# Hybrid decoder layer on one core: the weight loads on GpSimd's queue, and the 32x32 inverses on 128 partitions

## The chip, the cores and the metric

The kernel runs on one core of one Trainium2 chip, as a single launch. The metric is the device time of one execution in microseconds (us). Engine names are those of the profile: PE is TensorE (PEld its weight loads), DVE is VectorE, ACT is ScalarE, POOL is GpSimd, SP is SyncE. "SPq" and "POOLq" are the sequencers of SP and POOL, which issue DMAs in the order of their instruction streams.

## The reference

One layer over 2048 tokens of width 1024, in float32:

```python
h = _rmsnorm(x, norm1_w)
proj = h @ w_in                       # 2048 HGRN2 columns, then 1792 RWKV-7 columns
o_hg = _hgrn2_mixer(q_raw, f_raw, i_raw, g_raw, lb, norm_w)     # 4 heads of 128, chunks of 64
rw_p = rw_p + (_token_shift(rw_p) - rw_p) * rw_shift_mu
o_rw = _rwkv7_mixer(r, k, v, wd, ad, gd, ...)                   # 8 heads of 64
x = x + concat([o_hg, o_rw]) @ w_out
x = x + _conv_ffn(_rmsnorm(x, norm2_w), w_up, conv_w, conv_b, w_down)   # d_ff 2816
return _rmsnorm(x, final_norm_w)
```

RWKV-7 updates a 64x64 state per token, `S = S diag(w) + (S a) b^T + v k^T`. The kernel works it out in chunks of 64 tokens, which needs the inverse of a unit triangular matrix for each chunk and head. HGRN2 is a gated linear recurrence, `S = diag(f) S + k v^T`, also worked out in chunks.

## The kernel before, in words

Phase 1 (function `phase1`) goes from x to the mixers' outputs and through the output projection for the first three of four blocks of 512 tokens. Phase 2 takes the last block's projection and the ConvFFN. The change touches phase 1 alone.

Phase 1 weaves three generators into one program. `dense` does the projections: for each block, 30 jobs of 128 columns of `w_in` (tile `pj`, lines 259 to 261), each 8 steps along the contraction, and each step three matmuls, since a float32 product is made from a high and a low part (`mm3`, `split`). It also does the norms, and for blocks 0 to 2 `out_block`, the product with `w_out`. `rw_stream` runs eight "supers" (`rw_super`, one for each block and half of the RWKV heads). `hg_stream` runs sixteen HGRN units (`hg_unit`, one for each block and head). After each step of the two mixers, `fill` adds dense work to the program. A scheduler then fixes the order of the instructions on each engine when the program is built. On the chip each engine, and each queue of DMA issues, goes through its own list in order and waits where a semaphore tells it to.

Weights. In block 0 a job loads two 256 KB pieces of `w_in` (tile `wraw`, line 550, four buffers), ACT and DVE split them into `wh` and `wl` (lines 243 and 244, four buffers each), and the halves are stored in DRAM as `Win` by POOL's queue (line 553). In blocks 1 to 3 a job loads four pieces of `Win` back (line 557). `out_block` loads `w_out` in 256 KB pieces into the same four `wraw` buffers (tile `woraw`, line 382), and splits them. All these loads are issued by SP's queue, as are the small transfers below, the mixers' outputs `oT` of blocks 0 to 2 (lines 918 and 1039), and the loads and stores of x. The outputs of block 3 are issued by POOL's queue (`last_dma`).

The inverse. A super holds 64 triangular 32x32 blocks: two halves of heads (u), two chunks of a pair (e), two diagonal blocks of a chunk (q), four pairs (b), two heads (h). DVE leaves them in tile `M` (line 708). Eight DMAs of 32 KB write them to DRAM as `Ed` (line 721), and one reads them back with a matrix to each of 64 partitions (`E`, line 723). DVE inverts by forward substitution: 31 steps of a multiply and an add (lines 774 and 776, tiles `etmp` and `Ti`), in which row j is taken into the rows below, over j + 1 columns. DVE then makes a transposed copy `TiT` (line 781), both go to DRAM as `Td` (lines 780 and 782), and twelve DMAs read them back: four into `TZ` (line 792) and eight into `TTs` (line 789). That is 23 DMAs a super. PE uses the result in three stages of small matmuls: `z` (line 800), `z2` (line 813) and `qus` (line 826). From `qus` ACT copies Q into `M` and the rest into `UV`; then come line 851 (needs Q), lines 867 and 874 (need `UV`), the chain over chunks (line 885), and the end (lines 895 to 918).

The HGRN unit. `scaled(l)` runs for levels 0 to 6 with four DVE multiplications each (lines 944 to 949): the odd halves of q times `Pf`, the even halves of k times `Sf`, and the updates of `Sf` and `Pf`. `Sf` starts as ones (line 937). Lines 965 and 1007 are matmuls on what they make.

Of the kernel before, what the change touches and what calls it, by code (L numbers as in the profile page):

```python
# [18 lines left out]
P = 128  # L19
# [42 lines left out]
def tile_layer(ctx, tc, consts, x, norm1_w, w_in, hg_lb_logits, hg_norm_w, rw_shift_mu, rw_w0, rw_w2,  # L62
# [200 lines left out]
    def phase1(c1):  # L263
# [23 lines left out]

        done = {"rw1": 0, "rw2": 0, "hg": 0}
# [77 lines left out]
        def out_block(nb, oh=None, ol=None, then=None):  # L366


            for i2 in range(2):
                for dh in range(2):  # L370
                    accs = [bank("pj") for _ in range(2)]
                    for k in range(KD):
# [9 lines left out]
                        dma(raw, w_out[0, k * P:(k + 1) * P, dh * 512:dh * 512 + 512])  # L382
# [115 lines left out]
        def dense():  # L498
# [45 lines left out]
            def load(i):  # L544
                if i < len(cols) and i not in loaded:
                    ws, ct = [], cols[i] // P
                    for k2 in range(2):
                        if i < NCOL:
                            raw = wp.tile([P, 4, P], F32, tag="wraw", name="wraw", bufs=4)
                            dma(raw, w_in[0, k2 * 512:k2 * 512 + 512, cols[i]:cols[i] + P].rearrange("(k p) c -> p k c", p=P))  # L550
# [3 lines left out]
                        else:  # L554
                            ws.append(tuple(wp.tile([P, 4, P], F32R, tag="w" + c, name="w" + c, bufs=4) for c in "hl"))
                            for c in range(2):
                                dma(ws[k2][c].bitcast(F32), Win[ct][k2][c])
# [71 lines left out]
        def rw_super(nb, s_):  # L629
# [68 lines left out]
            for j in range(2):  # L698
                for u in U:
# [7 lines left out]
                    for h in range(2):  # L707
                        V.tensor_mul(M[:, u, :, 2 * j:2 * j + 2, h, :].rearrange("p e b t -> p b e t"),
                                     s1[:, h].rearrange("p (b e t) -> p b e t", e=2, t=P),
                                     s1m.unsqueeze(1).unsqueeze(1).broadcast_to([P, 2, 2, P]))  # L710
# [4 lines left out]
            Td = dp.tile([2, 64, 32, 32], F32, tag="Td", name="Td", bufs=2)  # L715
# [37 lines left out]
            for b, h, e, u in quads():  # L753
                kr, c0, sl = 64 - er0(e), col0(u, e), (b * 2 + h) * 64
                TE.matmul(lv[c0:c0 + 64, u, sl:sl + 64], M[kr:kr + 64, u, e, b, h, 0:64],
# [9 lines left out]
            n = 64  # L765
            Ti = rp.tile([P, 32, 32], F32, tag="Ti", name="Ti")
            V.memset(Ti[0:n], 0.0)
            V.memset(Ti[0:n].rearrange("m a b -> m (a b)")[:, 0:1024:33], 1.0)
            yield
            for j in range(31):  # L770
                nr, ncol = 31 - j, j + 1
                tmp = rp.tile([P, 272], F32, tag="etmp", name="etmp")
                tv = tmp[0:n, 0:nr * ncol].rearrange("m (a b) -> m a b", b=ncol)
                V.tensor_mul(tv, E[0:n, j, j + 1:32].unsqueeze(2).broadcast_to([n, nr, ncol]),
                             Ti[0:n, j, 0:ncol].unsqueeze(1).broadcast_to([n, nr, ncol]))
                V.tensor_add(Ti[0:n, j + 1:32, 0:ncol], Ti[0:n, j + 1:32, 0:ncol], tv)
                if j % 4 == 3:
                    yield
            TiT = rp.tile([P, 32, 32], F32, tag="E", name="TiT")
            dma(Td[0], Ti[0:n])  # L780
            V.tensor_copy(TiT[0:n], Ti[0:n].rearrange("m a b -> m b a"))
            dma(Td[1], TiT[0:n])
            TZ = tile_("XH", [2, 2, 4, 2, 32], "TZ")
            for u in U:
                for e in range(2):
                    r0 = er0(e)
# [5 lines left out]
                    dma(TZ[r0:r0 + 32, 0, u].rearrange("p b h t -> p (b h) t"),  # L792
                        Td[0, m0:m0 + 8].rearrange("m s t -> s m t"))
# [3 lines left out]
            for b, h, e, u in quads():  # L797
                r0 = er0(e)
                c0, sl = r0 + 32 - 32 * u, u * 256 + (b * 2 + h) * 32
                TE.matmul(z[c0:c0 + 32, 0, sl:sl + 32], M[r0:r0 + 32, u, e, b, h, 32:64],  # L800
# [705 lines left out]
```

## Time and profile before

| what | value |
|---|---|
| median of 3 runs (lowest to highest) | 2757.54 us (2757.54 to 2757.74) |
| the profiled execution: its time, its span | 2750.25 us, 2748.5 us |
| its mean granted TensorE clock | 0.982 |
| instructions | 47939 |

A view that groups instructions has line, engine, operation, names (out<-in) and count, then busy time in us and the mean ns of one, then the idle time before them and what ended it. A view of waits has who waited for whom, the total in us, the number of waits, and the longest. Each engine's busy time in a stretch is in us; "PEclk" there is the granted clock as a share of full speed. Line numbers are those of the kernel before; the changed kernel's are one to five higher.

### The profile page before, as it was taken

How to read it: one execution, taken by the hardware profiler on the slowest of the kernel's cores; microseconds unless marked ns; L12 is line 12 of the kernel's file. 1: busy time of each engine (PE TensorE's matmuls, PEld its weight loads, DVE VectorE, ACT ScalarE, POOL GpSimd, SP SyncE). 2: the span in 40 equal slices, each digit the busy share in tenths (PEclk: the TensorE clock that was granted, in tenths of full speed). 3: DMA queues.
4: the chain of work that ended last, by engine and by line, in shares of the span. 5: the costliest groups of instructions: out<-in, count | busy, mean ns of one | idle time of the engine just before them, and what ended most of it. 6: DMA issues, size and time to landing. Idle time of an engine off the chain costs nothing.

```text
span 2748.5 us, 47939 instructions
## 1 busy us (share of the span) xinstructions
PE 2645.1 (96%) x18059; PEld 2108.0 (77%) x18059; DVE 1964.0 (71%) x3697; ACT 1329.2 (48%) x2124; POOL 75.7 (3%) x144
## 2 busy tenths in 40 slices
PE   8999999989999899999989999998999999999998
PEld 6777777767777667778668788886888888777887
DVE  5868666585576765757567789988997787667656
ACT  5455342544534444343346754555545455445544
POOL 3211000000000000000000000000000000000000
PEclk9999999989999999999999999999999999999999
DMA  9555544345653456743584467746662224999865
GB/s 302 197 163 169 166 133 127 118 133 183 209 168 120 140 158 216 239 167 121 152 279 145 126 206 260 243 143 225 220 221 75 91 86 157 312 329 311 287 195 184
DMA packets 396029, 513.68 MB, mean 187 GB/s; under 512 B 73503, under 2 KB 200853, under 8 KB 395797
## 3 DMA queue, kind: packets, MB, share of 16 engines
q1 hardware_dynamic: 385137, 476.49, 53.9%
q0 software_dynamic: 10592, 34.11, 3.4%
q8 instruction: 142, 2.33, 0.4%
q14 instruction: 90, 0.74, 0.1%
q10 hardware_dynamic: 68, 0.02, 0.0%
HBM read 373.12 MB, written 137.36 MB: 186 GB/s over the span
## 4 chain that ended last, share of the span: by engine, by line
PE 60%; DVE 7%; DMA 5%; ACT 2%; issue 2%; SPq 1%; DVEq 0%; ACTq 0%
PE ua L261 5%; PE ua L259 5%; PE ua L260 5%; PE pj L259 5%; PE pj L260 4%; PE pj L261 4%; PE ud L259 3%; PE ud L260 3%; PE ud L261 3%; PE da L260 2%; PE da L261 2%; PE da L259 2%; PE db L260 2%; PE db L259 2%; PE db L261 2%
## 5 line engine op out<-in xcount | busy, mean ns | idle before, releaser
L259 PE MATMUL pj<-hh,wh 128*128 128x512 f32 x960 | 401.8, 419 | 0.8 <-DVE xh L398 0.6
L261 PE MATMUL pj<-hh,wl 128*128 128x512 f32 x960 | 379.7, 396 | 0.4 <-DMA wl<-Win191l 0.4
L260 PE MATMUL pj<-hl,wh 128*128 128x512 f32 x960 | 379.7, 396 | 0.0
L259 PE MATMUL ua<-Bh,uwh 128*128 128x512 f32 x704 | 278.7, 396 | 14.9 <-ACT uwh L243 14.1
L261 PE MATMUL ua<-Bh,uwl 128*128 128x512 f32 x704 | 276.3, 393 | 0.3 <-DVE uwl L244 0.3
L260 PE MATMUL ua<-Bl,uwh 128*128 128x512 f32 x704 | 276.1, 392 | 0.0
L259 PEld LDWEIGHTS pj<-hh,wh 128*128 128x128 f32 x960 | 181.3, 189 | 53.4 <-issue 12.4
L260 PEld LDWEIGHTS pj<-hl,wh 128*128 128x128 f32 x960 | 181.4, 189 | 40.3 <-issue 6.0
L261 PEld LDWEIGHTS pj<-hh,wl 128*128 128x128 f32 x960 | 180.9, 188 | 39.6 <-issue 0.7
L243 ACT CAST uwh<-uraw 128x512 fp32r<-128x512 f32 x220 | 134.5, 618 | 140.9 <-PE ua L260 71.4
L243 ACT CAST dah<-draw 128x512 fp32r<-128x512 f32 x151 | 93.8, 621 | 184.6 <-PE da L260 50.5
L244 DVE TENSOR_TENSOR uwl<-uraw,uwh 128x512 fp32r<-128x512 f32 x220 | 147.3, 688 | 46.9 <-ACT uwh L243 46.8
L244 DVE TENSOR_TENSOR dal<-draw,dah 128x512 fp32r<-128x512 f32 x151 | 104.3, 690 | 104.9 <-ACT dah L243 104.6
L259 PEld LDWEIGHTS ua<-Bh,uwh 128*128 128x128 f32 x704 | 133.4, 190 | 43.7 <-ACT uwh L243 14.7
L261 PEld LDWEIGHTS ua<-Bh,uwl 128*128 128x128 f32 x704 | 133.3, 189 | 30.1 <-DVE uwl L244 2.2
L260 PEld LDWEIGHTS ua<-Bl,uwh 128*128 128x128 f32 x704 | 133.7, 190 | 27.2
L259 PE MATMUL ud<-Bh,uwh 128*128 128x512 f32 x352 | 137.8, 392 | 1.9 <-DVE cv L1357 1.9
L261 PE MATMUL ud<-Bh,uwl 128*128 128x512 f32 x352 | 137.1, 389 | 0.0
L260 PE MATMUL ud<-Bl,uwh 128*128 128x512 f32 x352 | 137.0, 389 | 0.0
L260 PE MATMUL da<-dbl,dah 128*128 128x512 f32 x340 | 134.2, 395 | 0.7 <-DVE dbl L244 0.2
L261 PE MATMUL da<-dbh,dal 128*128 128x512 f32 x340 | 133.2, 392 | 0.0
L259 PE MATMUL da<-dbh,dah 128*128 128x512 f32 x340 | 128.3, 391 | 1.6 <-ACT dbh L243 1.5
(434 smaller groups left out, 5792.2 us busy)
## 6 DMA issues: line engine op xcount, KB each, us to landing
uraw<-in_w_up_dram SPq DMA_DIRECT2D x176, 256.0 KB, 3.2
woraw<-in_w_out_dram SPq DMA_DIRECT2D x96, 256.0 KB, 3.5
draw<-Sg SPq DMA_DIRECT2D x88, 256.0 KB, 3.5
draw<-Tw SPq DMA_DIRECT2D x88, 256.0 KB, 3.7
gd<-y SPq DMA_DIRECT2D x86, 256.0 KB, 2.9
xt<-x1d SPq DMA_DIRECT2D x32, 512.0 KB, 5.3
draw<-gd SPq DMA_DIRECT2D x63, 256.0 KB, 5.0
draw<-in_w_down_dram SPq DMA_DIRECT2D x63, 256.0 KB, 5.2
```

Source lines behind the costliest of these rows:

```text
L243: S.copy(hi, src)
L244: V.tensor_sub(lo, src, hi.bitcast(F32))
L259: TE.matmul(acc, lh, rh, start=first, stop=False, skip_group_check=skip)
L260: TE.matmul(acc, lh, rl, start=False, stop=False, skip_group_check=skip)
L261: TE.matmul(acc, ll, rh, start=False, stop=last, skip_group_check=skip)
```

## The change

It has four parts.

1. The loads of `w_in`, `Win` and `w_out` in phase 1 are issued by GpSimd's queue (`wload`) in place of SP's: 60 of `wraw`, 360 of `Win` and 96 of `woraw`.
2. The inverse runs on 128 partitions. Partitions 0 to 63 hold the even columns of the 64 inverses, partitions 64 to 127 the odd ones; `E` is loaded twice. A step still spans the same rows, but j // 2 + 1 columns in place of j + 1. `M` has its axes u and e exchanged, so that one DMA takes both u. There are 4 DMAs to `Ed`, 2 to `E`, 1 of `Ti`, 2 of `TiT`, 4 to `TZ`, 4 to `TTs`: 17 a super in place of 23. ACT makes the transposed copy in place of DVE.
3. After `qus`, ACT copies all of Q into `M` first, and then `UV`. Before, both were mixed.
4. In level 0 of an HGRN unit `Sf` is all ones, so two of the four multiplications are copies; ACT makes them. `Sf`'s memset writes half as many elements.

```diff
+        wload = nc.gpsimd.dma_start
...
-                        dma(raw, w_out[0, k * P:(k + 1) * P, dh * 512:dh * 512 + 512])
+                        wload(raw, w_out[0, k * P:(k + 1) * P, dh * 512:dh * 512 + 512])
...
-                            dma(raw, w_in[0, k2 * 512:k2 * 512 + 512, cols[i]:cols[i] + P].rearrange("(k p) c -> p k c", p=P))
+                            wload(raw, w_in[0, k2 * 512:k2 * 512 + 512, cols[i]:cols[i] + P].rearrange("(k p) c -> p k c", p=P))
...
-                                dma(ws[k2][c].bitcast(F32), Win[ct][k2][c])
+                                wload(ws[k2][c].bitcast(F32), Win[ct][k2][c])
...
-            for u in U:
-                for e in range(2):
-                    for q in range(2):
-                        r0 = er0(e) + 32 * q
-                        m0 = u * 32 + (e * 2 + q) * 8
-                        dma(Ed[m0:m0 + 8].rearrange("m s t -> s m t"),
-                            M[r0:r0 + 32, u, e, :, :, 32 * q:32 * q + 32].rearrange("p b h t -> p (b h) t"))
-            dma(E[0:64], Ed)
+            for e in range(2):
+                for q in range(2):
+                    r0 = er0(e) + 32 * q
+                    m0 = (e * 2 + q) * 16
+                    dma(Ed[m0:m0 + 16].rearrange("m s t -> s m t"),
+                        M[r0:r0 + 32, e, :, :, :, 32 * q:32 * q + 32].rearrange("p u b h t -> p (u b h) t"))
+            for f in range(2):
+                dma(E[64 * f:64 * f + 64], Ed)
...
             for j in range(31):
-                nr, ncol = 31 - j, j + 1
+                nr, ncol = 31 - j, j // 2 + 1
...
-                V.tensor_mul(tv, E[0:n, j, j + 1:32].unsqueeze(2).broadcast_to([n, nr, ncol]),
-                             Ti[0:n, j, 0:ncol].unsqueeze(1).broadcast_to([n, nr, ncol]))
-                V.tensor_add(Ti[0:n, j + 1:32, 0:ncol], Ti[0:n, j + 1:32, 0:ncol], tv)
+                V.tensor_mul(tv, E[:, j, j + 1:32].unsqueeze(2).broadcast_to([P, nr, ncol]),
+                             Ti[:, j, 0:ncol].unsqueeze(1).broadcast_to([P, nr, ncol]))
+                V.tensor_add(Ti[:, j + 1:32, 0:ncol], Ti[:, j + 1:32, 0:ncol], tv)
...
-            dma(Td[0], Ti[0:n])
-            V.tensor_copy(TiT[0:n], Ti[0:n].rearrange("m a b -> m b a"))
-            dma(Td[1], TiT[0:n])
+            dma(T0d.rearrange("f m t c -> (f m) t c"), Ti)
+            act(TiT, Ti.rearrange("m a b -> m b a"), AF.Copy)
+            for f in range(2):
+                dma(T1d[:, :, f, :], TiT[64 * f:64 * f + 64])
...
-                    for q in range(2):
-                        m0 = u * 32 + (e * 2 + q) * 8
-                        dma(TTs[r0 + 32 * q:r0 + 32 * q + 32, 8 * u:8 * u + 8, 32 * q:32 * q + 32],
-                            Td[1, m0:m0 + 8].rearrange("m s t -> s m t"))
-                    m0 = u * 32 + e * 16
-                    dma(TZ[r0:r0 + 32, 0, u].rearrange("p b h t -> p (b h) t"),
-                        Td[0, m0:m0 + 8].rearrange("m s t -> s m t"))
+                for f in range(2):
+                    dma(TZ[r0:r0 + 32, 0].rearrange("p u b h t -> p (u b h) t")[:, :, 16 * f:16 * f + 16],
+                        T0d[f, 32 * e:32 * e + 16].rearrange("m t c -> t m c"))
+                for q in range(2):
+                    m0 = (e * 2 + q) * 16
+                    dma(TTs[r0 + 32 * q:r0 + 32 * q + 32, :, 32 * q:32 * q + 32],
+                        T1d[m0:m0 + 16].rearrange("m c f t -> (c f) m t"))
...
-                if u == 0:
-                    act(M[:, u, 0, :, :, 0:64], quv[:, :, :, 0:64], AF.Copy)
+            act(M[:, 0, 0, :, :, 0:64], quv[0][:, :, :, 0:64], AF.Copy)
+            for e in range(2):
+                r0, c0 = er0(e), col0(1, e)
+                act(M[r0:r0 + 64, 0, 1, :, :, 0:64], quv[1][c0:c0 + 64, :, :, 0:64], AF.Copy)
...
-            V.memset(Sf, 1.0)
+            V.memset(Sf.rearrange("p (n e) -> p n e", e=2)[:, :, 1:2], 1.0)
...
-                V.tensor_mul(vw(X)[:, :, 0, :], vw(k)[:, :, 0, :], vw(Sf)[:, :, 0, :])
...
+                if l == 0:
+                    act(vw(X)[:, :, 0, :], vw(k)[:, :, 0, :], AF.Copy)
+                    act(vw(Sf)[:, :, 0, :], vw(Pf)[:, :, 1, :], AF.Copy)
```

The scheduler places everything anew. Three places show what that does.

SP's list around the inverse of the second super, before: the loads of weights (`wh`, `wl` from `Win`) stand among the inverse's transfers.

```order
L557 DMA wl<-Win200l 128x512
L408 DMA xt<-in_x_dram 128x1024
L780 DMA Td<-Ti 64x1024
L782 DMA Td<-TiT 64x1024
L557 DMA wh<-Win201h 128x512
L792 DMA TZ<-Td 32x8x32 x2
L789 DMA TTs<-Td 32x8x32 x6
L792 DMA TZ<-Td 32x8x32
L789 DMA TTs<-Td 32x8x32 x2
L792 DMA TZ<-Td 32x8x32
L1039 DMA oT_142<-osq 128x512
L557 DMA wl<-Win201l 128x512
```

The same place of SP's list after the change.

```order
L725 DMA E<-Ed 64x1024 x2
L409 DMA xt<-in_x_dram 128x1024 x4
L782 DMA T0d<-Ti 128x512
L785 DMA T1d<-TiT 1024x1x32 x2
L790 DMA TZ<-T0d 32x16x16 x3
L794 DMA TTs<-T1d 32x16x32 x2
L790 DMA TZ<-T0d 32x16x16
L794 DMA TTs<-T1d 32x16x32 x2
L1044 DMA oT_142<-osq 128x512
```

No weight stands there any more, and the last `TZ` is the sixth of eight reads where it was the last of twelve.

ACT's list after `qus` of the first super, before.

```order
L117 ACTIVATE M<-rw 128x8x64
L117 ACTIVATE UV<-rw 64x4x128 x2
L117 ACTIVATE M<-rw 64x8x64
L117 ACTIVATE UV<-rw 64x4x128
L117 ACTIVATE M<-rw 64x8x64
L117 ACTIVATE UV<-rw 64x4x128
```

And after the change (`nsq` and `nst` belong to the norm of a later block).

```order
L117 ACTIVATE nsq,nst<-xt 128x1024
L117 ACTIVATE M<-rw 128x8x64
L117 ACTIVATE M<-rw 64x8x64 x2
L117 ACTIVATE UV<-rw 64x4x128 x4
L117 ACTIVATE nst<-nst 128x1
L117 ACTIVATE nst<-nst,eps_73 128x1
```

The last copy into `M` has moved from the sixth place to the third.

ACT's list around the inverse of the third super after the change (`sgm` is a sigmoid on a projection's result, `hf` the HGRN gate, `osq` the end of an HGRN unit, `gdt` a projection's result). Before, `Sf<-hf` and `TiT<-Ti` were DVE's.

```order
L117 ACTIVATE sgm<-pj 128x512
L117 ACTIVATE Sf<-hf 128x256
L117 ACTIVATE osq<-hg 128x512
L117 ACTIVATE TiT<-Ti 128x512
L117 ACTIVATE gdt<-pj,omu 128x512
```

Two instructions that wait for DVE now stand in ACT's list among those that empty PSUM for PE.

PE's list is the same from the last super's line 903 on, and so in all of phase 2.

More of the change, by code (lines that the diff above doesn't have):

```diff
@@ L777, in rw_super @@
                 if j % 4 == 3:
                     yield
[L779 to L782, printed above, removed]
-            TZ = tile_("XH", [2, 2, 4, 2, 32], "TZ")
-            for u in U:
-                for e in range(2):
-                    r0 = er0(e)
-                    for q in range(2):
-                        m0 = u * 32 + (e * 2 + q) * 8
-                        dma(TTs[r0 + 32 * q:r0 + 32 * q + 32, 8 * u:8 * u + 8, 32 * q:32 * q + 32],
-                            Td[1, m0:m0 + 8].rearrange("m s t -> s m t"))
-                    m0 = u * 32 + e * 16
-                    dma(TZ[r0:r0 + 32, 0, u].rearrange("p b h t -> p (b h) t"),
-                        Td[0, m0:m0 + 8].rearrange("m s t -> s m t"))
+            TiT = rp.tile([P, 16, 32], F32, tag="E", name="TiT")
@@ new lines, in rw_super @@
+            dma(T0d.rearrange("f m t c -> (f m) t c"), Ti)
+            act(TiT, Ti.rearrange("m a b -> m b a"), AF.Copy)
+            for f in range(2):
+                dma(T1d[:, :, f, :], TiT[64 * f:64 * f + 64])
+            TZ = tile_("XH", [2, 2, 4, 2, 32], "TZ")
+            for e in range(2):
+                r0 = er0(e)
+                for f in range(2):
+                    dma(TZ[r0:r0 + 32, 0].rearrange("p u b h t -> p (u b h) t")[:, :, 16 * f:16 * f + 16],
[4 more added lines that the diff above has]
+                        T1d[m0:m0 + 16].rearrange("m c f t -> (c f) m t"))
@@ L884, in rw_super @@
                         hr = slice(h * 64, h * 64 + 64)
-                        TE.matmul(xp[hr, u, cs_], M[hr, u, 1, b, e, 0:64], XH[hr, u, ch, :], start=False,
+                        TE.matmul(xp[hr, u, cs_], M[hr, 1, u, b, e, 0:64], XH[hr, u, ch, :], start=False,
                                   stop=ch == 7, tile_position=(h * 64, h * 64), skip_group_check=True)
```

46 lines of the change are left out of this document (23 added, 23 removed).

## The prediction

> **What bounds the kernel now.** I read the page first, then stretches, then PE's waits.
>
> The page's first part gives busy time by engine, with the share of the span.
>
> ```profile
> PE 2645.1 (96%) x18059; PEld 2108.0 (77%) x18059; DVE 1964.0 (71%) x3697; ACT 1329.2 (48%) x2124; POOL 75.7 (3%) x144
> ```
>
> PE is the bound, and the change takes no matmul away. So only two things can be won: time in which PE waits, and time in which its clock is granted at less than full speed. The view by stretches says where. Its columns are the stretch, its length, busy time of PE, PEld, DVE, ACT and POOL, then the granted clock, the DMA share and GB/s. The first two rows are phase 1 and phase 2. The others are those stretches around the stages z, z2 and qus in which the clock fell.
>
> ```profile
> 0.00:1390.00 1390.00, 1318.14 (x12257) 1021.58 (x12257) 906.69 (x2103) 615.08 (x983) 74.59 (x142) 0.98 0.53 169
> 1390.00:2748.00 1358.00, 1326.96 (x5802) 1086.45 (x5802) 1057.29 (x1595) 714.13 (x1142) 1.09 (x2) 0.99 0.62 205
> ...
> 290.00:320.00 30.00, 28.17 (x453) 22.16 (x451) 17.91 (x49) 16.11 (x31) 0.00 (x0) 0.89 0.66 211
> 585.00:625.00 40.00, 31.13 (x577) 24.26 (x577) 28.01 (x68) 14.78 (x30) 0.00 (x0) 0.79 0.46 133
> 935.00:975.00 40.00, 31.24 (x517) 22.89 (x516) 23.86 (x55) 17.68 (x33) 0.00 (x0) 0.83 0.56 159
> 1155.00:1195.00 40.00, 36.82 (x641) 28.36 (x640) 27.91 (x65) 11.78 (x23) 0.54 (x1) 0.83 0.63 205
> 1310.00:1350.00 40.00, 33.37 (x628) 26.80 (x625) 24.55 (x60) 15.91 (x33) 0.00 (x0) 0.87 0.41 114
> ```
>
> In phase 1 PE is idle for 1390 - 1318 = 72 us. The five slow stretches lose 30 x 0.11 + 40 x (0.21 + 0.17 + 0.17 + 0.13) = 30 us of full clock. Together 102 us, 3.7% of the span, is all that the change can reach. PE's waits in phase 1 (who waits for what, total us, times, longest) divide the 72:
>
> ```profile
> PE vps L151 <- DMA rows<-in_hg_lb_logits_dram: 9.5, 1, 9.5
> PE rw L800 <- DMA TZ<-Td: 7.6, 5, 3.4
> PE hg L1007 <- DVE hk L1000: 6.6, 5, 2.8
> PE pj L259 <- ACT wh L243: 5.7, 5, 1.8
> PE rw L851 <- ACT UV L117: 5.7, 7, 1.0
> PE hg L965 <- DVE hX L944: 4.8, 7, 1.2
> PE hg L965 <- DVE hX L945: 3.3, 2, 1.9
> PE rw L867 <- DVE AR L857: 3.2, 3, 1.4
> PE pj L260 <- DVE wl L244: 3.1, 4, 1.9
> ```
>
> The first is the start of the program. The second is the inverse: z waits for what comes back from DRAM. The HGRN rows (hk, hX) and AR wait for DVE. The pj rows wait for the splits of weights, that is, behind their loads. The rest of the 72 us lies in waits of at most 2 us in all per row and in gaps too short for this view; I leave it as it is.
>
> **The inverse: z.** These rows show DVE's groups; the third and fourth are two sizes of one step, the fifth the transposed copy.
>
> ```profile
> L776 DVE TENSOR_TENSOR Ti<-Ti,etmp 64x31 f32<-64x31 f32 (+15 forms) x248 | 82.8, 334 | 3.7
> L774 DVE TENSOR_TENSOR etmp<-E,Ti 64x31 f32<-64x31 f32 (+15 forms) x248 | 82.6, 333 | 45.5 <-DMA E<-Ed 42.1
> ...
> L776 DVE TENSOR_TENSOR Ti<-Ti,etmp 64x255 f32<-64x255 f32 x16 | 6.6, 415 | 0.1
> L776 DVE TENSOR_TENSOR Ti<-Ti,etmp 64x60 f32<-64x60 f32 x16 | 3.4, 213 | 0.4
> L781 DVE COPY TiT<-Ti 64x1024 f32<-64x1024 f32 x8 | 8.6, 1080 | 0.2
> ```
>
> Between 60 and 255 elements the time grows by (415 - 213) / 195 = 1.04 ns an element, on 151 ns that every instruction pays. A super's 62 instructions now go over 2 x 5456 elements a partition: 62 x 0.151 + 10912 x 0.00104 = 20.7 us, which is the measured (82.8 + 82.6) / 8. With j // 2 + 1 columns it is 2 x 2856 elements: 9.4 + 5.9 = 15.3 us. The halving takes 5.4 us and not 10, since the 151 ns stay. Then SP's reads, here from the second super:
>
> ```profile
> 291.11 0.46 SPq L780 DMA_DIRECT2D Td<-Ti  x1
> 292.26 0.45 SPq L782 DMA_DIRECT2D Td<-TiT  x1
> 292.80 0.54 SPq L557 DMA_DIRECT2D wh<-Win201h  x1
> 295.99 0.82 SPq L792 DMA_DIRECT2D TZ<-Td  x2
> ...
> 301.30 0.45 SPq L792 DMA_DIRECT2D TZ<-Td  x1
> ```
>
> Twelve issues take 301.75 - 295.99 = 5.8 us, 0.48 each, and z needs the last of them. Where it is the sixth, 2.9 us go. Against that, E and TiT each have one more DMA on the chain, 0.5 us each by the same pace. What TiT costs on ACT is bounded by ACT's 128x512 copies of `KT` (0.59 us, quoted below) and DVE's 1.08, so I count nothing. The chain into z gets 5.4 + 2.9 - 1.0 = 7.3 us shorter, and the longest wait there is 3.4. The order keeps z's place or puts it slightly earlier, so I take 6.5 of the 7.6 us, with 3 and 7.6 as ends. What is late next at z is the copy of TZ on ACT between z and z2, unchanged. On the front side DVE's first step still stands 42.1 us in all for E, since the last Ed leaves at the same time.
>
> **ACT's order after qus.** Line 851's second half needs the last copy into M, which was sixth and is third. The 5.7 us should nearly go: 4.5, with 2 and 5.7 as ends. Lines 867 and 874 need UV, which is still complete with the seventh copy; they stand behind DVE's adds on what 851 makes (the AR row), so that costs nothing as long as those adds end later.
>
> **DVE's relief.** Off DVE come 8 x 5.4 = 43 us, 8.6 of TiT, and 32 multiplications in level 0; on to ACT come 40 copies.
>
> ```profile
> L945 DVE TENSOR_TENSOR hX<-hk,Sf 128x256 f32<-128x256 f32 x112 | 47.1, 420 | 0.2
> ...
> L117 ACT ACTIVATE KT<-hg 128x512 f32<-128x512 f32 x16 | 9.5, 593 | 12.1 <-PE hg L1007 12.0
> L236 ACT CAST hh<-oraw 128x256 fp32r<-128x256 f32 x8 | 3.2, 403 | 3.7 <-DMA oraw<-oT 3.6
> ```
>
> That is 32 x 0.42 = 13 us, so 65 of DVE's 907 us, 7%. ACT gains 8 x 0.59 + 32 x 0.40 = 18 us on 615. PE waits 6.6 + 4.8 + 3.3 + 3.2 = 18 us for DVE on the HGRN and AR rows, but each of these is a dependence within one unit, where a quarter at most falls away with a less crowded DVE: 4 us, with 0 and 10 as ends.
>
> **The queues.** How long POOL takes to issue, and from issue to landing (us, at the end of a row):
>
> ```profile
> L1039 POOL DMA_DIRECT2D oT<-osq x4 | 2.2, 545 | 1045.7 <-DVE osq L1038 966.5 <-DVE etmp L774 75.0 <-DVE lastc L302 4.2
> L918 POOL DMA_DIRECT2D oT<-yo x2 | 1.4, 716 | 67.1 <-issue 67.1
> ...
> woraw<-in_w_out_dram SPq DMA_DIRECT2D x96, 256.0 KB, 3.5
> oT<-osq SPq DMA_DIRECT2D x12, 256.0 KB, 3.8
> oT<-osq POOLq DMA_DIRECT2D x4, 256.0 KB, 2.4
> ```
>
> From SP these 256 KB stores land after 3.8 us, from POOL after 2.4, issue included. No row shows a load from POOL; I take it to land as from SP. The `wraw` loads have four runs a partition; yo's transfer with twice the runs costs 0.17 us more, so 0.55 + 3 x 0.17 = 1.1 us. A column in block 0 then takes 2 x 1.1 + 4 x 0.55 = 4.4 us of POOL. The page's slices, 68.7 us each, show how long POOL's stores of block 0 last:
>
> ```profile
> POOL 3211000000000000000000000000000000000000
> ```
>
> Four slices, 275 us, for 30 jobs leave 9 us a job, so POOL keeps up. SP was
>
> ```profile
> SPq L557 <- PE pj L261: 484.2, 156, 15.5
> ```
>
> waiting for a weight buffer for 484 us, and whatever stood behind that in its list waited too. With the weights gone, the inverse, xh and oT leave when they are ready. Behind a waiting weight on POOL now stand only other weights, the Win stores, and block 3's outputs. I take 2 of the 8.8 us on the pj rows, with -5 (later) and 7 as ends.
>
> **The clock.** The slow periods follow z, z2 and qus, where PE has small matmuls and gaps. Three of the eight supers have none. With z's and 851's gaps mostly gone I count 4 of the 30 us, with -6 and 15 as ends.
>
> **Costs.** TiT and the copies of level 0 wait in ACT's list for DVE, with casts of `wh` and evictions behind them. SP's list has waited for Ti so far, at the place of the first store of the result:
>
> ```profile
> SPq L780 <- DVE Ti L776: 9.7, 7, 3.1
> ```
>
> At the same 1.4 us a super ACT would stand 11 us; I put 3 of them on PE, from 0 to 10. The start has wraw ahead of `rows` on POOL, one issue of 1.1 us, on the path of the 9.5 us: 1 us.
>
> Sum: -6.5 - 4.5 - 4 - 2 - 4 + 3 + 1 = -17 us. The profiled execution took 2750.25 us with a span of 2748.5, 7.3 under the median of the runs, 2757.54. Its waits stand for theirs, so the forecast is 2757.5 - 17 = 2740.5 us, with 2725 to 2753 as its own range.
>
> **The rivals.**
>
> *PE's idle time only moves* (0.14): the order is new, and gaps close in one place and open in another. For: 72 us of idle time come from some thirty kinds of waits. Against: both removed waits are dependences that really get shorter. Time: 2757, the terms eaten by new ones.
>
> *DVE now waits for ACT* (0.14, the other side). In level 1 DVE needs `Sf` from ACT's copy, and ACT takes its list in order:
>
> ```profile
> ACT rkv L117 <- PE pj L261: 108.5, 24, 14.7
> ```
>
> A wait there is 108.5 / 24 = 4.5 us. Were each of the 16 units' DVE steps held so long, DVE would lose 72 us; with half of it reaching PE, 36 us against the 21 won: 2757.5 - 21 + 36 = 2772. It decides from 21 / 16 = 1.3 us on PE a unit. Against: f is ready long before level 0 needs it, and `Sf` often stands right behind its sigmoid.
>
> *GpSimd issues late* (0.07). The one kind of DVE instruction that I can put beside it is
>
> ```profile
> L415 DVE TENSOR_SCALAR xt<-xt,nst 128x1024 f32<-128x1024 f32 x20 | 14.3, 748 | 0.0
> ```
>
> If each issue stood behind such a 0.75 us, and took 0.2 longer than SP's, the 96 woraw loads, in rounds of four buffers, would lose 24 x 1 us, and the 2 us on the pj rows would not come: 2740.5 + 26 = 2767. Against: POOL's issues of 545 ns hardly vary beside a busy DVE. [...]
>
> *The clock recovers whole* (0.08): all 30 us return, so 26 more than counted: 2714. For: the gaps at z go. Against: three supers kept their clock with the same stages. [...]
>
> **How the numbers follow.** The forecast has 0.57. A measurement of this kernel tells about 0.2%, 5.5 us, from no change. Of the forecast's own range 0.53 lies below 2752 and 0.04 within 0.2%. Faster: 0.53 + 0.08 + 0.02 of the first rival = 0.63. Same: 0.04 + 0.10 + 0.01 = 0.15. Slower: 0.02 + 0.13 + 0.07 = 0.22. The range reaches from 2716 to 2769: it holds the forecast, the first rival, GpSimd's and half of ACT's, and leaves out about 0.15.
>
> **What would show it.** Right: no wait of z for TZ above 1 us, 851's wait under 2 us, etmp and Ti at about 247 and 246 ns a piece, SP's wait for PE gone and POOL's in its place, phase 2 still 1358 us. Wrong: waits of PE for `wh` or `wl` that end with a DMA from POOL, a new wait of DVE for ACT's `Sf`, or POOL's issues well over 0.55 us for `Win` and 1.1 for `wraw`.

## The result and the profile after

The changed kernel takes 2755.64 us in the median of 20 runs (2746.56 to 2763.78), the kernel before 2757.64 us in 20 runs beside it (2751.43 to 2765.61). The ratio is 0.9988, with a 95% interval of 0.9978 to 0.9997: 3.3 us less by the ratio (2.0 by the medians), where 17 were forecast. Single executions of either kernel lie up to 9 us off its median. The profiled execution of before lay 7 us under its median, that of after 2 us above its own, so the two spans (2748.5 and 2755.7 us) cannot be subtracted. Rows can be compared.

The page's first part, and phase 1, which here ends at 1398 us instead of 1390:

```profile
PE 2647.8 (96%) x18059; PEld 2107.5 (76%) x18059; DVE 1898.6 (69%) x3665; ACT 1350.4 (49%) x2164; POOL 368.3 (13%) x660
```

```profile
0.00:1398.00 1398.00, 1320.10 (x12258) 1020.78 (x12259) 843.25 (x2072) 635.99 (x1023) 367.21 (x658) 0.98 0.54 170
```

Over the program DVE lost 65 us (1964.0 to 1898.6) and ACT gained 21 (1329.2 to 1350.4), where 65 and 18 were worked out beforehand. PE's idle time in phase 1 is 78 us (1398 - 1320) after 72, so in these executions nothing of the 72 was won. In both, 7 us of it stand just ahead of phase 2's first matmul, a gap that the list of waits in the prediction ended too early to show. The granted clock of this stretch is 0.98 as before; the other executions come below. PE's waits in phase 1 (who for whom, total us, times, longest) show where the gain went:

```profile
PE pj L259 <- ACT wh L243: 14.7, 12, 4.3
PE rw L802 <- DMA TZ<-T0d: 14.3, 9, 4.3
PE vps L151 <- DMA cst<-in_consts_dram: 11.0, 1, 11.0
PE rw L868 <- DVE AR L858: 8.9, 6, 2.2
...
PE rw L852 <- ACT UV L117: 0.7, 2, 0.6
```

Line 851 (now 852) has all but left the list, and so have the hX rows. But z's wait for TZ, which was to go, rose from 7.6 to 14.3 us. The wait for `wh` rose from 5.7 to 14.7, and the AR row from 3.2 to 8.9. The inverse itself became as short as forecast; its two groups on DVE:

```profile
L778 DVE TENSOR_TENSOR Ti<-Ti,etmp 128x126 f32<-128x126 f32 (+22 forms) x248 | 62.4, 252 | 3.5
L776 DVE TENSOR_TENSOR etmp<-E,Ti 128x126 f32<-128x126 f32 (+22 forms) x248 | 61.8, 249 | 15.5 <-DMA E<-Ed 12.2
```

252 and 249 ns a piece, against 246 and 247 worked out. So the parts must be taken one by one.

### The profile page after: what moved, and what is told of

Read it like the earlier page. It is cut to its first block, busy times and chain, and to the rows that moved or that the text cites. A ratio compares the mean times of both kernels' runs of the same rounds, so it can differ in the third digit from the quotient of the medians.

```text
span 2755.7 us, 47958 instructions
## 1 busy us (share of the span) xinstructions
PE 2647.8 (96%) x18059; PEld 2107.5 (76%) x18059; DVE 1898.6 (69%) x3665; ACT 1350.4 (49%) x2164; POOL 368.3 (13%) x660
## 4 chain that ended last, share of the span: by engine, by line
PE 73%; DMA 8%; DVE 7%; issue 5%; ACT 4%; SPq 1%; POOL 1%; DVEq 0%; ACTq 0%; POOLq 0%
PE pj L259 8%; PE pj L260 7%; PE pj L261 7%; PE ua L261 5%; PE ua L259 5%; PE ua L260 5%; PE ud L259 3%; PE ud L260 3%; PE ud L261 3%; PE da L260 2%; PE da L261 2%; PE da L259 2%; PE hg L970 2%; PE db L259 2%; PE db L261 2%
```

## The experiments

Letters for the parts: W the weight loads on GpSimd's queue, I the inverse, C the copies of level 0 on ACT, O ACT's order after qus. Theory in short: some parts won, and others gave it back. Rival: PE's idle time only moves, whatever part is applied. Each edit also goes through the scheduler again: in `p_wload`, PE's list has another matmul than before (by names and sizes) at 2989 of its 18059 places, in `r_win` another than in `q_invorder` at 1419. No run changes a part and keeps the order, so a price below is that of an edit with the order that came with it. A time in us is the ratio less one, times 2757. "Chain" is worked out from the records: from the issue of the first Ed to z's first matmul, mean of the eight supers of the profiled execution. In before, in the first super, they are the issue at 91.68 and the matmul at 149.51:

```profile
91.68 0.95 SPq L721 DMA_DIRECT2D Ed<-M  x2
```

```profile
149.51 0.24 PE L800 MATMUL rw<-TZ,M 32*32 32x32 f32 x2 [1.56 <-DMA TZ<-Td]
```

That is 57.8 us, and over eight supers 56.6. "Clock" is the granted clock, the median of all executions of a kernel; the kernel before has 0.980 or 0.981 in each group of runs. In the traces of the two kernels it has only two values, full and half: in before it is half in twelve stretches of 3.4 to 17.1 us, among them 955 to 957 us (0.50 in a view of that stretch), and full in all others; 0.001 of the mean is 2.8 us that are not granted. How much of such time is lost is not known, since some of it falls on PE's idle time. All runs:

| kernel | parts | ratio to before (95%) | us | chain, us | clock |
|---|---|---|---|---|---|
| changed | W I C O | 0.9988 (0.9978 to 0.9997) | -3 | 53.2 | 0.986 |
| p_wload | W | 1.0089 (1.0076 to 1.0102) | +25 | 60.0 | 0.980 |
| p_inv | I | 0.9948 (0.9933 to 0.9963) | -14 | 51.2 | 0.984 |
| p_copies | C | 1.0041 (1.0028 to 1.0054) | +11 | 56.3 | 0.980 |
| p_order | O | 0.9994 (0.9985 to 1.0002) | -2 | 56.9 | 0.982 |
| q_invorder | I O | 0.9935 (0.9923 to 0.9948) | -18 | 51.3 | 0.983 |
| q_nowload | I C O | 0.9960 (0.9948 to 0.9972) | -11 | 50.7 | 0.983 |
| q_nocopies | W I O | 0.9985 (0.9972 to 0.9997) | -4 | 53.5 | 0.986 |
| q_noorder | W I C | 0.9998 (0.9987 to 1.0008) | -1 | 53.1 | 0.984 |
| r_win | I O, Win of W | 0.9930 (0.9916 to 0.9945) | -19 | 52.9 | 0.987 |
| r_woraw | I O, woraw of W | 0.9973 (0.9960 to 0.9987) | -7 | 52.3 | 0.985 |
| r_wraw | I O, wraw of W | 0.9940 (0.9927 to 0.9953) | -17 | 51.3 | 0.984 |
| r_x | I O, k's copy of C | 0.9952 (0.9934 to 0.9969) | -13 | 51.5 | 0.983 |
| s_padin | I O, DVE time added in the chain | 1.0087 (1.0073 to 1.0101) | +24 | 63.0 | 0.975 |
| s_padout | I O, the same behind it | 0.9957 (0.9943 to 0.9970) | -12 | 51.4 | 0.984 |
| s_b5 | I O, five raw buffers | 0.9919 (0.9906 to 0.9932) | -22 | 51.9 | 0.981 |
| s_b5w | s_b5, woraw of W | 0.9922 (0.9903 to 0.9940) | -22 | 53.0 | 0.986 |
| t_bwin | Win of W | 1.0057 (1.0042 to 1.0072) | +16 | 58.5 | 0.980 |
| t_best | s_b5, TZ read first | 0.9880 (0.9866 to 0.9895) | -33 | 51.9 | 0.983 |

### One part at a time

**W alone** (the `wload` lines of the diff above):

> The kernel before with only the weight loads (wraw, woraw, and wh and wl from Win) on GpSimd's queue. Theory 1 (the parts add, and this one costs): the first wait of PE becomes 11 us instead of 9.5, PE's waits for wh rise from 5.7 to about 14 us in phase 1 as in the changed kernel, and the time rises by 6 to 12 us, to about 2766. Theory 2 (PE's idle time only moves between rows): within 3 us of before. What the forecast said of it: 1 us later at the start, 2 earlier at the pj rows.

25 us slower, more than either theory had, and the chain is 3.4 us longer. PE's waits in phase 1, and the reads of TTs and TZ (issues, KB, median us from issue to landing):

```profile
PE rw L801 <- DMA TZ<-Td: 21.0, 7, 6.7
PE pj L259 <- ACT wh L243: 12.0, 10, 2.2
```

```profile
TTs<-Td SPq DMA_DIRECT2D x64, 32.0 KB, 4.4
TZ<-Td SPq DMA_DIRECT2D x32, 32.0 KB, 3.4
```

Before it was 1.9 and 2.2 us:

```profile
TTs<-Td SPq DMA_DIRECT2D x64, 32.0 KB, 1.9
TZ<-Td SPq DMA_DIRECT2D x32, 32.0 KB, 2.2
```

SP issues the small reads nearly as before (0.486 us each on average, 0.466 before); they land later. By the order of the lists, a weight load on SP stood behind the inverse's waiting store, and so moved at another time than the reads; on its own queue it moves beside them. The records show it: in the 3 us before a small read is issued, 0.1 weight loads are issued on average in the kernel before, and 1.2 in `p_wload`. The clearest case is `r_win` below, with Win's loads alone on GpSimd's queue. In its second, third, fifth and seventh super 1.4 to 2.1 weight loads stand in those 3 us, and the reads whose landing is recorded take 2.6 to 6.2 us; in the fourth, sixth and eighth none does, and they take 2.1 to 2.6. (The first super's are slow in any case: 3.7 and 4.1 us in `q_invorder`, with no weight load in those 3 us.)

**I alone** (the diff's lines on Ed, E, Ti, TiT, TZ and TTs):

> The kernel before with only the inverse on 128 partitions with 17 transfers (with the copy of TiT on ACT and M in its new axis order). Theory 1: from the first Ed to z is 3 to 4 us shorter a super, not 7, since an issue of the finer reads takes 0.8 us instead of 0.45 and the two loads of E take 2.6 us longer; the wait of z for TZ falls from 7.6 us to under 4, and the time falls by about 3 us, to 2755. Theory 2: the wait of z stays at 7 us or rises as in the changed kernel (14.3), and the time is within 3 us of before. The forecast: 6.5 us from z's wait and some of the 4 us from DVE's relief, about 2748.

14 us faster, although z's wait hardly fell:

```profile
PE rw L802 <- DMA TZ<-T0d: 7.3, 5, 2.2
```

Both theories were wrong. The mean issue of a TZ or TTs read is 0.473 us (0.466 before, 0.486 with W alone, 0.609 in the changed kernel), so neither the finer read nor W alone makes the issue slow, but both together. That z's row stays while the kernel gets 14 us faster says that the row is no price of the chain. A part of the 14 us can be clock: 0.984 after 0.981, 8 us that are granted in addition. Two runs below take this up.

**C alone:**

```diff
-                V.tensor_mul(vw(X)[:, :, 0, :], vw(k)[:, :, 0, :], vw(Sf)[:, :, 0, :])
...
+                if l == 0:
+                    act(vw(X)[:, :, 0, :], vw(k)[:, :, 0, :], AF.Copy)
+                    act(vw(Sf)[:, :, 0, :], vw(Pf)[:, :, 1, :], AF.Copy)
```

> The kernel before with only level 0 of HGRN by copies on ACT. Theory 1: DVE is 13 us less busy, the two hX rows of PE's waits (4.8 + 3.3 us) go, and the time falls by about 3 us, to 2755. Theory 2: the hX rows go and others take their place, within 3 us of before. Rival of the forecast (DVE waits for ACT's Sf): slower by 5 us or more, with a new wait of DVE for ACT's Sf.

11 us slower, and no wait of DVE for ACT's Sf. The rival's cost came, but by another way: ACT's list stands.

```profile
ACT hX L117 <- DVE hk L926: 13.9, 9, 5.5
ACT Sf L117 <- PE hg L1022: 10.6, 8, 2.2
ACT Sf L117 <- DVE hf L341: 5.3, 4, 1.8
```

30 us in which ACT stands at a copy, with evictions and casts behind it in its list: for hk, for the matmuls that still read the unit before's Sf, and for hf. On PE two waits for what ACT makes are up, from 5.7 us each:

```profile
PE rw L851 <- ACT UV L117: 8.0, 10, 1.0
PE pj L259 <- ACT wh L243: 7.7, 7, 2.0
```

That is 4 of the 11 us.

**O alone:**

```diff
+            act(M[:, 0, 0, :, :, 0:64], quv[0][:, :, :, 0:64], AF.Copy)
+            for e in range(2):
+                r0, c0 = er0(e), col0(1, e)
+                act(M[r0:r0 + 64, 1, 0, :, :, 0:64], quv[1][c0:c0 + 64, :, :, 0:64], AF.Copy)
```

> The kernel before with only ACT's new order after qus (the three copies into M ahead of the four into UV). Theory 1: the wait of line 851 (5.7 us) falls under 1 us, the wait of line 867 rises from 3.2 to about 6 us (8.9 in the changed kernel), and the time falls by about 2 to 3 us. Theory 2: 867 takes all of what 851 gives back: no change. The forecast: 4.5 us less, to 2753.

2 us, with an interval from 4 faster to 1 slower. Line 851's row went, and the AR row took more than half of it (3.2 to 6.5 us):

```profile
PE rw L866 <- DVE AR L856: 6.5, 6, 1.8
```

The rival of all four falls here: three parts alone move the time itself, by 11 to 25 us, and not only PE's idle time from row to row.

### Parts together

The first two put the weights back on SP, the first and third undo C, the last undoes O:

```diff
-        wload = nc.gpsimd.dma_start
+        wload = dma
```

> The changed kernel without the weight loads on GpSimd's queue and without the copies of level 0 on ACT: the inverse and ACT's new order, the two parts that alone did not cost. If the parts add (14.5 us less for the inverse, 1.7 for the order), the ratio is 0.994 and the time 2741 us. If the order only hands its wait on to line 868, 2743, as with the inverse alone. Line 852's wait, 7.3 us with the inverse alone, falls under 1 us, and 868's rises.

18 us faster. I and O add up (14 and 2), within what the runs can tell.

> The changed kernel with the weight loads back on SP. Theory 1 (the parts add): 2757 - 14.5 + 10 - 1.7 = 2751 us. Theory 2 (the copies cost only while DVE's long inverse holds ACT's list; with the short inverse they cost nothing): 2741. Theory 3 (the queue's cost is what the short inverse takes away, the copies keep theirs): 2751 too, and then the changed kernel without the copies is the fast one. Issues of TZ and TTs go back from 0.61 us to 0.47 on average.

11 us faster, so C costs 7 us beside I and O. Theory 2 falls. The mean issue of a TZ or TTs read is 0.479 us, as expected.

> The changed kernel with level 0's multiplications back on DVE. Theory 1 (the parts add): 2757 + 24 - 14.5 - 1.7 = 2765 us. Theory 2 (the copies cost nothing beside the short inverse, the queue costs about 14 us): 2756 as the changed kernel. Theory 3 (the queue costs nothing beside the short inverse, the copies 10): 2745. The row of ACT's wait for hk (13.9 us with the copies alone) goes in each case.

4 us faster: W costs 14 us beside I and O, and C nearly nothing on top of W (1 us). The 14 is net of a higher clock, 0.986 after 0.983. As theory 2 had it for the time, but not for its reason, as `q_nowload` shows: C costs where W is not.

> The changed kernel with ACT's old order after qus. Line 851's wait (0.7 us in the changed kernel) comes back to 5 to 7 us, and that of 868 falls from 8.9 to 3 us. Parts that add: 1.7 us slower than the changed kernel, 2757. The forecast had 4.5 us for it: 2760.

1 us faster than before, so O is worth some 3 us here too, with intervals that overlap.

### Which weight loads

On I and O, one of the three loads at a time, here for Win; in `r_x` only the copy into X is made by ACT:

```diff
-                                dma(ws[k2][c].bitcast(F32), Win[ct][k2][c])
+                                nc.gpsimd.dma_start(ws[k2][c].bitcast(F32), Win[ct][k2][c])
```

> The inverse and ACT's new order (2741 us), with only the reads of Win (wh and wl of blocks 1 to 3, 168 of them) on GpSimd's queue. All weight loads on that queue cost 14 us on this base (0.9985 against 0.9935). Theory B (the weights, which stood behind the inverse's stores and reads in SP's list, now move while those move): most of the cost is here, 7 to 12 us, z's wait for TZ rises from 7.5 us to 11 or more and a read of TTs takes 3.5 us or more from issue to landing instead of 2.5. Theory Q (late is what stands behind other weights in GpSimd's list, woraw above all): under 3 us here.

(The edit moves all 360 reads, not 168.) Theory B's wait came, and its cost did not; a read of TTs lands after 2.5 us as without it, and one of TZ after 3.9 instead of 2.9:

```profile
PE rw L802 <- DMA TZ<-T0d: 13.4, 7, 3.2
```

z's wait went from 7.5 to 13.4 us at no cost. Phase 1 of both, by stretches (q_invorder first; the last columns are the granted clock, the DMA share, GB/s):

```profile
0.00:1382.00 1382.00, 1315.25 (x12257) 1023.37 (x12257) 858.15 (x2103) 624.80 (x991) 74.60 (x142) 0.98 0.55 172
```

```profile
0.00:1384.00 1384.00, 1310.58 (x12257) 1015.12 (x12257) 856.95 (x2103) 622.53 (x991) 268.95 (x502) 0.99 0.55 171
```

PE was idle 73 us instead of 67, and was granted 0.99 instead of 0.98 of its clock. That is 7 us more idle time and 5 us less busy time for the same matmuls. It is no accident of one execution: the five of `r_win` were granted 0.986 to 0.988 of the clock, the five of `q_invorder` 0.982 to 0.985. So Win's loads seem to have a cost here that the clock pays back; the idle time is known of one execution each. Why the clock is higher with them stays open.

> The same base with only the 96 woraw loads on GpSimd's queue, so that no Win read stands ahead of them there. Theory B: they move beside the inverse of the last supers only, 1 to 4 us slower than 2741. Theory Q: no cost either, as nothing waiting for PE stands ahead of them; then only the whole change costs. A cost of 7 us or more here would mean that woraw itself comes later by this queue: PE's wait for wh up from 6.5 us to 10 or more.

11 us slower than `q_invorder`. ACT's wait for woraw (q_invorder, then r_woraw):

```profile
ACT wh L243 <- DMA woraw<-in_w_out_dram: 32.4, 20, 4.5
```

```profile
ACT wh L243 <- DMA woraw<-in_w_out_dram: 58.3, 37, 4.9
```

No other weight load stands in GpSimd's list here, so it is the load itself. One turn of the buffer on SP (q_invorder): DVE's split ends at 628.66, the next load is issued at 628.69.

```profile
627.98 0.68 DVE L244 TENSOR_TENSOR wl<-woraw,wh 128x512 fp32r<-128x512 f32 x1
```

```profile
628.69 0.33 SPq L383 DMA_DIRECT2D woraw<-in_w_out_dram  x1
```

The same on GpSimd (r_woraw): 634.04, and 634.34. (The row names another instruction of DVE that ended about then; 0.295 us behind the split is where most of the 96 issues lie.)

```profile
633.35 0.69 DVE L244 TENSOR_TENSOR wl<-woraw,wh 128x512 fp32r<-128x512 f32 x1 [1.87 <-ACT wh L243]
```

```profile
634.34 0.54 POOL L383 DMA_DIRECT2D woraw<-in_w_out_dram  x1 [2.23 <-DVE XH L888]
```

Over all loads the median from a split's end to the next issue is 0.027 us on SP and 0.295 on GpSimd, and the shortest from issue to split 2.57 and 2.86 us: 0.56 us a turn. 96 loads through four buffers make 24 turns, some 13 us; 11 came. A part can be the reads': z's wait is 9.1 us after 7.5, and the chain 1.0 us longer.

> The same base with only the 60 wraw loads of block 0 on GpSimd's queue, among the stores to Win. PE's first wait goes from 9.8 to 11 us and the second load of the first column is late by some 3 us: 2 to 4 us slower than 2741 by either theory, and z's wait in the first super alone is up.

1 us slower than `q_invorder`, within what the runs can tell. PE's first wait, 10.8 us, is up as expected.

> The inverse and ACT's new order, with only the copy of k into X in level 0 on ACT, the copy into Sf left as a multiplication on DVE. Both copies cost 7 us on this base (2748 against 2741). If the cost is ACT's list standing for DVE's hk (9 to 14 us with both), 4 us or more of it is here; if it is Sf's copy, which stands for the matmuls of the unit before (9 to 10 us) and for hf (5), this kernel is within 2 us of 2741.

5 us of C's 7 come with the copy of k alone, and with them ACT's wait for hk:

```profile
ACT hX L117 <- DVE hk L927: 14.7, 7, 4.7
```

The interval (3 us on either side) leaves room for Sf's part.

### What bounds, and what the ring does

The same DVE work inside the chain (first) and behind the first store (second):

```diff
-                V.tensor_mul(tv, E[:, j, j + 1:32]...
+                for _ in range(2 if 4 <= j < 26 else 1):
+                    V.tensor_mul(tv, E[:, j, j + 1:32]...
```

```diff
             dma(T0d.rearrange("f m t c -> (f m) t c"), Ti)
+            for j in range(4, 26):
+                ...
+                V.tensor_mul(tmp[:, 0:nr * ncol]..., Ti[:, j + 1:32, 0:ncol], Ti[:, j, 0:ncol]...
```

> The inverse and ACT's new order (2741 us), with 22 of the inverse's 31 multiplications done twice in each super: about 5.5 us of DVE put back inside the chain into z. Theory K (the inverse won by its shorter chain): some 10 us slower, 2751. Theory D (it won because DVE is less full, wherever): the same as with the padding outside the chain. Theory T (it won by 17 transfers instead of 25): under 3 us slower in both.

> The same base with 22 multiplications of the same sizes put on DVE right behind the first store of the result, outside the chain into z: the same 5.5 us of DVE a super. Theory K: under 4 us slower than 2741. Theory D: some 10 us slower, as with the padding inside. Theory T: under 3 us in both.

Inside the chain it cost 42 us over `q_invorder`, outside 6. The group of the steps in s_padin, and the group of the padding in s_padout:

```profile
L777 DVE TENSOR_TENSOR etmp<-E,Ti 128x126 f32<-128x126 f32 (+22 forms) x424 | 110.0, 259 | 19.2 <-DMA E<-Ed 14.0
```

```profile
L786 DVE TENSOR_TENSOR etmp<-Ti 128x126 f32<-128x126 f32 (+15 forms) x176 | 48.2, 274 | 4.0
```

Without padding `q_invorder` has 62.7, so 47 us were added in the first, 48.2 in the second: the same work. Theory K had the place right, and the size inside wrong (10 us, not 42); theories D and T fall. A reason why the place decides is seen in DVE's busy time. Sums over the eight stretches from the inverse's first multiplication to its last addition, and then over the eight from there to z's end, in the kernel before; and over the first eight in q_invorder:

```profile
sum 300.20, PE 293.83 PEld 239.23 DVE 282.00 ACT 115.74 POOL 14.55; mean PE 36.73 PEld 29.90 DVE 35.25 ACT 14.47 POOL 1.82
sum 121.30, PE 101.92 PEld 78.71 DVE 83.39 ACT 37.49 POOL 5.94; mean PE 12.74 PEld 9.84 DVE 10.42 ACT 4.69 POOL 0.74
...
sum 257.80, PE 257.16 PEld 212.01 DVE 233.06 ACT 91.24 POOL 13.03; mean PE 32.15 PEld 26.50 DVE 29.13 ACT 11.41 POOL 1.63
```

In the first DVE is busy 282 of 300 us, 94%, and in `q_invorder` 233 of 258, 90%, with other units' work between the steps of the inverse. So time added there lengthens the super. (PE is busy too, 257 of 258 us: it pays later, when the work that it filled the time with is used up. That is argued from the rows, not shown.) In `s_padin` the stretches grew to 349 us, by 91 for 47 of padding: DVE is busy 317 us in them, so 37 us of other units' work came between the steps as well. Behind the inverse DVE has room; with the padding outside it goes from 52 of 100 us (q_invorder, first) to 84 of 98 (s_padout):

```profile
sum 99.80, PE 85.08 PEld 64.52 DVE 52.34 ACT 44.75 POOL 5.39; mean PE 10.63 PEld 8.07 DVE 6.54 ACT 5.59 POOL 0.67
```

```profile
sum 98.30, PE 82.32 PEld 61.48 DVE 84.48 ACT 44.33 POOL 5.40; mean PE 10.29 PEld 7.69 DVE 10.56 ACT 5.54 POOL 0.67
```

The chain's price is not even. From 51.3 to 56.6 us (I taken away) 14 us, 0.33 for each of the 8 x 5.3 us; from 51.3 to 63.0 (padding) 42 us, so 28 us for the last 8 x 6.4, 0.55 each. In s_padin z's own wait is 2.4 us, the smallest of all: the loss stands in other rows and in the clock, 0.96 granted in phase 1. By the last row below and q_invorder's above, PE is idle for 88 us after 67, and busy for 1338 us after 1315 with the same matmuls: half of the 44 us is idle time, half goes with the clock.

```profile
PE rw L869 <- DVE AR L859: 11.0, 6, 2.3
...
PE rw L803 <- DMA TZ<-T0d: 2.4, 2, 1.8
```

```profile
0.00:1426.00 1426.00, 1337.78 (x12257) 1038.59 (x12257) 891.32 (x2278) 624.97 (x990) 74.58 (x142) 0.96 0.53 166
```

The ring of raw buffers (every tile of that tag gets a fifth), without and with woraw on GpSimd's queue:

```diff
-                        raw = wp.tile([P, 512], F32, tag="wraw", name="woraw", bufs=4)
+                        raw = wp.tile([P, 512], F32, tag="wraw", name="woraw", bufs=5)
```

> The same base with five buffers instead of four for the raw weights (wraw, woraw, xh, oraw). If the ring of woraw buffers bounds the output projections, ACT's wait for woraw falls from 32 us to under 20, PE's wait for wh from 6.5 us to under 4, and the time by 3 to 6 us to 2737. If not, 2741.

> Five buffers, and the woraw loads on GpSimd's queue. With four buffers these loads cost 9 to 10 us. Theory R (each turn of the ring is 0.57 us longer: GpSimd issues 0.30 us after DVE frees a buffer where SP needs 0.03, and its shortest issue to split is 2.86 us against 2.57): a fifth buffer covers it, and this is within 4 us of the kernel with five buffers and SP. Theory M (GpSimd's transfers take their cost from the transfers beside them): still 9 to 10 us slower.

Five buffers win 4 us over `q_invorder`, and ACT's wait for woraw falls from 32.4 to 17.5 us. With woraw on GpSimd it is 26.8, and the time the same (0.9922 against 0.9919).

```profile
ACT wh L243 <- DMA woraw<-in_w_out_dram: 17.5, 15, 2.9
```

```profile
ACT wh L243 <- DMA woraw<-in_w_out_dram: 26.8, 16, 2.6
```

The time is as theory R had it. PE's waits are not: the one for `wh` comes back with woraw on GpSimd (s_b5, then s_b5w), and z's goes from 4.9 to 8.7 us.

```profile
PE pj L259 <- ACT wh L243: 1.1, 3, 0.4
...
PE pj L259 <- ACT wh L243: 7.6, 9, 2.9
```

And the clock is higher, 0.986 after 0.981. So the longer turn of the ring is measured and has the size of woraw's 11 us, but the fifth buffer does not show that it is all of them: here too the clock may hide a cost.

Win's loads alone on the kernel before (the edit of `r_win`):

> The kernel before, long inverse and all, with only the reads of Win on GpSimd's queue. On the short inverse they cost nothing (2741.2 against 2741.4), though z's wait rose from 7.5 to 13.4 us. Theory K (the chain from Ed to z has slack beside PE's other work, some of it left with the short inverse and none with the long): here the chain grows from 56.6 us to 59 or 60, and the time by 10 to 15 us to 2770; with the 9 to 10 us of woraw that makes the 24 of all weight loads. Rival: Win costs nothing here either, and the 24 us come from all loads together.

16 us slower, the chain 1.9 us longer: Win's loads cost nothing in time beside the short inverse and 16 us beside the long one, as theory K had it. With woraw's 11 this makes 27, and W's cost is 25 us. But that theory K's slack is the reason is not shown. The chain's price does not give the size (8 x 1.9 us at 0.55 would be 8), and the clock differs: it stays at 0.980 here, where `r_win` was granted 0.987 after 0.983.

**The version the runs point to:**

```diff
             for e in range(2):
                 r0 = er0(e)
                 for f in range(2):
                     dma(TZ[r0:r0 + 32, 0]...
+            for e in range(2):
+                r0 = er0(e)
                 for q in range(2):
                     m0 = (e * 2 + q) * 16
                     dma(TTs[...
```

> Five raw buffers, the inverse, ACT's new order, weights on SP (2735.5 us), and the four reads of TZ issued ahead of the four of TTs instead of between them. z needs the fourth read instead of the sixth: about 1 us of chain a super; z's wait falls from 4.9 us to under 3. By the slope of this end (14 us for 8 x 5.3 us of chain) 2 to 3 us: 2733. Rival: TTs, later by 1 us, takes it back at z2: 2735.5.

2726.45 us, 33 less than before and 30 less than the changed kernel by the ratios. z's wait is 3.3 us after 4.9 (under 3 was expected), and the wait for TTs that the rival feared is 0.7.

```profile
PE rw L804 <- DMA TZ<-T0d: 3.3, 4, 1.5
...
PE rw L817 <- DMA TTs<-T1d: 0.7, 1, 0.7
```

That is 11 us more than `s_b5`, where 2 to 3 were expected. Its phase 1 was also denied less of the clock (26 us after 40 in the profiled executions; 0.983 after 0.981 over all). Whether the order of eight reads gives this or the clock's moments fell well was not settled.

## Why the prediction was right or wrong

The direction was right, by 3.3 us, and the time lay within the wide range (2716 to 2769), above the forecast's own (2725 to 2753). The sum was wrong. That I and O alone come to -18, close to the -17, is chance: the sum had -11 for the two, and -6 for the other terms. What the forecast lacked were the costs of W and C.

**The queues (-2) were the step that failed.** W cost 14 us beside I and O, 25 on the kernel before. The step saw that GpSimd keeps up and that weights would no longer hold SP's list. It did not see that this very hold kept the weights apart from the inverse's reads (they landed after 4.4 and 3.4 us with W, 1.9 and 2.2 before), nor that each turn of woraw's ring gets longer (0.56 us). The latter comes close to the rival "GpSimd issues late", given 0.07, with its 24 rounds; it priced a round at 1 us and dismissed it because GpSimd's issues of 545 ns hardly vary. Nor did they in the changed kernel, where woraw's 96 took 537 to 539 ns. What was late was not the issue (538 ns) but its start, 0.27 us, with 0.29 more to the split.

**DVE's relief (-4) and ACT's list (+3)** are the second failure. DVE did lose the 13 us by C, and 3 more (1964.0 to 1947.8 us in `p_copies`), but as relief that was worth less than ACT's standing: 30 us for three kinds of waits. The step reckoned 11, all of it from the wait for Ti, and had no figure for the waits of level 0's copies. C cost 11 us alone and 7 beside I and O; it cost 1 on top of W.

**The inverse (-6.5)** had the right working and the wrong end. The steps went from 37.5 to 32.2 us of wall time, 5.3 (worked out: 5.4), and from the first store to the last issue of TZ it went from 10.1 to 7.0 us (in `p_inv`; 8.4 in the changed kernel). The term was then capped by z's wait, 7.6 us. I gained 14, at a nearly unchanged wait (7.3 us). The cap took a wait's length for the price of the chain that ends there.

**ACT's order (-4.5)**: the wait at 851 went from 5.7 to 0.7 us as forecast. The condition set beside it, that the adds into AR end later anyway, did not hold: the AR row rose, and 2 to 4 us were left.

**The clock (-4)** hardly shows in the profiled executions: 49 us not granted after, 51 before. But over all executions the changed kernel was granted 0.986 and the kernel before 0.981, which is 14 us. So this term came, perhaps with more than was counted; how much of it was time gained is not known. The prices above are net of it. **The start (+1)** was right: 9.5 to 11.0 us. Phase 2 was unchanged, as forecast. Of the marks named for "wrong", longer waits of PE for `wh` came (14.7 us), by way of ACT's split and not straight from a DMA; a wait of DVE for Sf did not, and GpSimd's issues stayed at 0.55 us for `Win` and 0.77 for `wraw`. Of those named for "right", z's longest wait for TZ was 4.3 us where none above 1 was to be.

## What to carry to other kernels

A transfer that waits in a shared queue may be keeping out of another's way: here the reads of TTs landed after 1.9 us with the weights in their queue and after 4.4 without. So before it gets its own queue, look at what will then move at the same time, and at how many buffers its ring has, since here each turn of woraw's ring got 0.56 us longer on the new queue. The price of a chain is not the wait at its end: taking 5.3 us a super out of it won 14 us at an unchanged wait, and the same DVE work cost 42 us inside it, where DVE was 90% busy, and 6 behind it. The clock has to be read over all executions: the profiled ones gave 0.983 after 0.982, all of them 0.986 after 0.981. And a copy given to an engine with time to spare (ACT, busy 48% of the span) can cost by what that engine stands for in its list: here ACT stood 30 us at the copies, and the kernel got 11 us slower where DVE lost 16 us of work.

## What was not expected of the hardware

Between the split that frees a buffer and the next `woraw` load's issue lay 0.295 us on GpSimd's queue (`r_woraw`) and 0.027 us on SP's (`q_invorder`), in the median of 96 loads. A `wraw` load, four runs a partition, took GpSimd 766 ns to issue in the changed kernel, a plain 256 KB `woraw` load 538. And a longer wait came with a higher granted clock and an unchanged time: with Win's loads on GpSimd's queue PE was idle 7 us longer in phase 1 (one execution each), the clock was 0.987 instead of 0.983 over five executions each, and the ratios are 0.9930 and 0.9935.
